# Attention's end reordered: a fourth home for residual rows, the last blocks' values behind more mixing steps, and turned v issued by GpSimd

## The chip, the cores and the metric

One core of a Trainium2 chip. The time is device microseconds (us) of one launch of the whole kernel. Engines are named as in the profile: PE (TensorE), DVE (VectorE), ACT (ScalarE), POOL (GpSimd), SP (SyncE, which here issues nearly all DMAs). "L76" is line 76 of the kernel.

## The reference

A trunk of two layers on one sequence of 1024 tokens, width 1024, in float32. Layer 0 mixes with a gated MLP and a gated delta rule; layer 1 with differential attention of 8 heads. The part around which the change lies, cut to what matters:

```python
h = h + concatenate([a_out, b_out]) @ w_out_e        # layer 0's mixing; then MLP and gate
...
q, k, v = split(rms_norm(h) @ w_qkv)                 # layer 1: 8 heads, two score maps each
attn = softmax(q1 k1) - lam * softmax(q2 k2)         # causal, with linear position bias
o = rms_norm(attn @ v, sub_gain) * (1 - lam_init)    # per head and token
h = h + o @ w_out_o                                  # the output projection ("mixing")
h = h + square(relu(rms_norm(h) @ w_mlp1)) @ w_mlp2  # then the gate
```

## The kernel before, in words

Every large product is made from float32 values split in a rounded part `hi` and a rest `lo`, so each product of a 128x128 weight block with 512 tokens is three PE matmuls (`mm3`): hi x hi, hi x lo, lo x hi. ScalarE makes `hi` (a cast), VectorE or GpSimd makes `lo` (a subtraction). Tokens are handled in two halves of 512.

**Order of the work.** The code issues instructions in program order; a planner then orders each engine's queue from its own model of times, by priority (program order, unless `high_priority` lifts a stretch of code) among what it takes to be ready. On the chip each queue runs strictly in that order, and waits where an operand is not there. `Ordered` (L40) wraps PE: `behind(inst, mark)` forces an instruction to come after another in the plan, `pe.floor` puts all matmuls issued while it is set behind a mark, and `pe.mark` is the last matmul issued. A Tile pool hands out memory by tag: a new tile of a tag waits until the last one in that home is done with.

**Attention** (`attention`, L887) runs 64 blocks, g = 8 x head + b, block b having b + 1 key tiles of 128. In turn g it issues block g's first map of scores (`logits(0)`), then for block g-1 the sum of both maps (`combine`, L1051 on VectorE) and `transpose` (L1056 on VectorE, 32x32 squares, then a DMA on SP to `a_dram`, L1058), for block g-2 `fetch` (L1067: one or two DMAs on SP that read `a_dram` back as `aT` with the squares in place), then `logits(1)`, and for block g-3 `value` (PE matmuls `po<-v,aT`). `value` ends with ScalarE copies (L1078, L1080) and, after every fourth block, the length factor of four blocks: small VectorE operations (L1087 to L1090: `osq`) and three GpSimd ones (L1092 to L1094). For heads 0 to 6 the scaled rows go to DRAM (`o_dram`); head 7's stay.

Between these parts `pump()` is called four times a turn. It draws the projections for later heads from a stream, and from the 206th call on one step of `tails()`. That generator turns six heads' rows of a token half (`put_halves`, `put_o`: PE transposes `tr<-ident,ol`, ScalarE `ohi` L1104, VectorE `olo` L1105), then runs `mix_part` for that half: the output projection over the first KA = 6 (half 0) or 5 (half 1) heads. `mix_part` makes 8 slices m of 128 output features, each 3 matmuls per head, and yields after every second head. It closes slice m behind the second head of slice m+1: VectorE adds the residual rows `res` (L1219), a DMA writes them to `h_dram` (L1220), and the load of slice m+2's rows is issued (L1209) into the next home, three homes in turn: tiles `c0`, `c1`, `c4`. What is left of `tails()` after turn 65 is drawn at once, then head 7's first half is turned.

`attention` returns two functions, kept in `close`: block 63's `value`, and the turning of head 7's second half. The top level then calls `mix_out` (L1237) for half 0 over the heads left (2 heads x 3 x 8 slices), pops the first function after step 8 (slice 3) and the second after step 16 (slice 7), and calls `mix_out` for half 1 (3 heads, of which heads 5 and 6 go first in slices 0 and 1). Each finished slice is added to `acc`, read from `h_dram` (L1249, L1266), squared by ScalarE (the first into the tile `sqs0` for half 0, L237) and summed by VectorE (L241). PSUM tiles of these products come from the tags in `wide`, two tiles each: `mm` and `tr`. The MLP follows.

**Turned v** (`turn`, L1399, layer 0): the values for the delta rule are transposed in 32x32 squares by VectorE (L1402) and written token by token to DRAM in four DMAs of 64 KB on ScalarE's queue (L1405); `(i, hf) == (2, 1)` is v's second half. `read_tokens` (L1411) reads them on SP for the scan's chunks.

Of the kernel before, what the change touches and what calls it, by code (L numbers as in the profile page):

```python
# [11 lines left out]
F32 = mybir.dt.float32  # L12
F32R = mybir.dt.float32r
AF = mybir.ActivationFunctionType
ALU = mybir.AluOpType
# [3 lines left out]
P = 128  # L19
D = 1024  # L20
S = 1024
KT = D // P
NT = S // P
HT = 512
# [5 lines left out]
EARLY = 3000  # L30
LAG = 3
KA = (6, 5)
MARKS = ((64, 50), (192, 144), (212, 160), (227, 168))
TAIL = 205
FILLA, FILLB, FILLC = 36, 60, 48
IDLE = 5
FILLS = (23, 23, 23, 23, 28, 28, 28, 28)
# [2 lines left out]
def f32(ap):  # L40
    return ap.bitcast(F32)
# [73 lines left out]
class Trunk:  # L115
# [771 lines left out]
    def attention(self, w_qkv, w_out, gain_next, h_dram):  # L887

        nc = self.nc
        NB = NT  # L890
        hs, r = list(self.hs), list(self.r)
        self.mixed = [[None] * KT, [None] * KT]
        self.res_home = itertools.cycle(("c0", "c1", "c4"))

        al = self.slot("B", [P, S], F32, "al")
        nc.gpsimd.iota(al, pattern=[[1, S]], base=-(S - P), channel_multiplier=-1, allow_small_or_imprecise_dtypes=True)
# [115 lines left out]
        class Block:  # L1012
# [40 lines left out]
            def transpose(me):  # L1053

                n, nk = me.n, me.b + 1
                nc.vector.transpose(me.lg[0][:, :n], me.lg[1][:, :n])  # L1056
                a_dram = self.dp.tile([nk, P, P], F32, name=self.nm("a_dram"))
                nc.sync.dma_start(a_dram.rearrange("k p c -> p k c"), me.lg[0][:, :n].rearrange("p (k c) -> p k c", c=P))  # L1058
                me.src = a_dram.rearrange("k (i r) (j c) -> k (r j) i c", r=32, c=32)

            def fetch(me):
                nk = me.b + 1
                me.aT = []
                for k0 in range(0, nk, 4):
                    k1 = min(nk, k0 + 4)
                    aT = self.attn_tile(next(aT_tag))
                    self.pe.behind(nc.sync.dma_start(aT[:, : (k1 - k0) * P].rearrange("p (k i c) -> p k i c", i=4, c=32), me.src[k0:k1].rearrange("k p i c -> p k i c")), self.pe.mark)  # L1067
                    me.aT.append(aT)
# [29 lines left out]
        def put_o(hd, hf, o):  # L1098
            pt = self.aux([P, HT], "tr", "tr")
            for t in range(4):  # L1100
                self.pe.transpose(pt[:, t * P : (t + 1) * P], o[:, t, :], self.ident)
            hi = self.hp.tile([P, HT], F32R, tag=f"hi{hf}{hd}", name=self.nm("ohi"))
            lo = self.hp.tile([P, HT], F32R, tag=f"lo{hf}{hd}", name=self.nm("olo"))
            nc.scalar.activation(hi, pt, AF.Copy, scale=self.sg)  # L1104
            nc.vector.scalar_tensor_tensor(lo, pt, self.sg, f32(hi), ALU.mult, ALU.subtract)  # L1105
            self.mixed[hf][hd] = (hi, lo)

        def put_halves():
# [17 lines left out]
        qks, vs, os = [[] for _ in range(8)], [], [[] for _ in range(8)]  # L1126
# [14 lines left out]
        def pump():  # L1141
            i = state[0] = state[0] + 1
            for (i0, u0), (i1, u1) in zip(marks, marks[1:]):
                if i0 < i <= i1:
                    want = u0 + (u1 - u0) * (i - i0) / (i1 - i0)
                    while state[1] < want:
                        next(fill)
                        state[1] += 1
            if i > TAIL:
                next(tail, None)  # L1150
# [11 lines left out]
            yield from puts  # L1162

        tail = tails()
        blocks = []
        for g in range(8 * NB + 2):
            if g < 8 * NB:
                hd, b = divmod(g, NB)
                blocks.append(Block(hd, b))
                blocks[g].logits(0)  # L1170
            if 0 < g <= 8 * NB:
                blocks[g - 1].combine()
                blocks[g - 1].transpose()
            pump()
            if 1 < g <= 8 * NB:
                blocks[g - 2].fetch()
            if g < 8 * NB and b % 2 and b < NB - 1:
                q = heads[hd][2]((b + 1) // 2)
            pump()
            if g < 8 * NB:  # L1180
                if b == 3 - (hd < 7):
                    heads[hd][1](1)
                blocks[g].logits(1)
            pump()
            if g == 8 * NB:
                blocks[g - 1].fetch()
            if g > 2:
                blocks[g - 3].value()
            pump()
            if g < 8 * NB:  # L1190
                if b % 2 and b < NB - 1:
                    heads[hd][3] = q
                if b == 6 and hd < 7:
                    begin(hd + 1)
        for _ in tail:
            pass
        put_o(7, 0, os[7][0])

        return blocks[8 * NB - 1].value, lambda: put_o(7, 1, os[7][1])


    def mix_part(self, h, n, w_out, h_dram):
        nc = self.nc
        cols = slice(h * HT, (h + 1) * HT)

        def load(m):
            if m < KT:
                res = self.slot(next(self.res_home), [P, HT], F32, "res")
                nc.sync.dma_start(res, h_dram[m, :, cols])  # L1209
                ahead.append(res)  # L1210

        ahead, open_ = [], []
        load(0)
        load(1)

        def close():
            m, ps = open_.pop(0)
            res = ahead.pop(0)
            self.pe.behind(nc.vector.tensor_tensor(res, res, ps, ALU.add), self.pe.mark)  # L1219
            nc.sync.dma_start(h_dram[m, :, cols], res)  # L1220
            load(m + 2)

        for m in range(KT):
            if m % 2 == 0:
                w = self.weight(w_out[0 : n * P, m * P : (m + 2) * P], n, 256, nc.gpsimd)
            ps = self.mm_ps()
            for k in range(n):
                self.mm3(ps, w.at(k, slice((m % 2) * P, (m % 2 + 1) * P)), self.mixed[h][k], k == 0, k == n - 1)
                if m and k == 1:
                    close()  # L1230
                if k % 2:
                    yield
            open_.append((m, ps))
        close()
# [65 lines left out]
    def even_mix(self, first, rows_of_rest, rest_of_x, w_in, ws, bs, conv, a_log, dt_bias, v_gain, o_gain, masks, w_out, gain_next, h_dram):  # L1300
        nc = self.nc
# [20 lines left out]
        hs, r, rb = self.hs, self.r, self.rb  # L1322
# [23 lines left out]
        hb, beta, g = small["hb"], small["beta"], small["g"]  # L1346
# [46 lines left out]
        qkv, made, by_token = {}, set(), {}  # L1393
# [5 lines left out]
        def turn(i, hf, m, y):  # L1399

            t = self.sp.tile([P, HT], F32, tag=f"sqs{m % 2}", name=self.nm("turned"), bufs=1)
            nc.vector.transpose(t, y)  # L1402
            for a in range(4):
                f0 = m * P + 32 * a
                nc.scalar.dma_start(by_token[i, hf].rearrange("(t c) f -> c t f", c=32)[:, :, f0 : f0 + 32], t[32 * a : 32 * a + 32].rearrange("c (t r) -> c t r", r=32))  # L1405

        def read_tokens(i, c, out):

# [539 lines left out]
        f0 = prep(0)  # L1948
# [16 lines left out]
def trunk(tc, x, p, ln_mix_e, w_in_e, gmlp_v_gain, gmlp_ws, gmlp_bs, gdn_conv, gdn_a_log, gdn_dt_bias, gdn_out_gain,  # L1965
          w_out_e, ln_mix_o, w_qkv_o, attn_q_gain, attn_k_gain, diff_lambda, attn_sub_gain, w_out_o, ln_mlp, w_mlp1,
          w_mlp2, ln_ple, w_ple_gate, w_ple_proj, masks, out):
    with ExitStack() as ctx:
        T = Trunk(tc, ctx)
        nc = tc.nc  # L1970
# [25 lines left out]
        pt = T.aux_ps()  # L1996
# [24 lines left out]
        T.even_mix(first, rows_of_rest, rest, w_in_e[0], gmlp_ws[0], cols[:, 96:100], conv, gdn_a_log[0], gdn_dt_bias[0], gmlp_v_gain[0], gdn_out_gain[0], masks, w_out_e[0], gain[1], h_dram)  # L2021
        T.attn_consts(attn_q_gain[0], attn_k_gain[0], diff_lambda[0], attn_sub_gain[0], lam_init)
        for layer in range(2):
            T.wide = ("mm", "tr")
            accs = [None] * 4

            def acc_of(m, h):
                i = 2 * h + m // 4
                if accs[i] is None:
                    accs[i] = T.slot(f"A{i ^ 2 * layer}", [P, 4, HT], F32, "acc")  # L2030
                return accs[i][:, m % 4]


            if layer:
                T.new_hs()
                for n, _ in enumerate(T.mix_out(0, lambda m: acc_of(m, 0), w_out_o[0], h_dram, gain[4], KA[0])):
                    if n + 1 in (4 * (KT - KA[0]), 8 * (KT - KA[0])):
                        close.pop(0)()
            for _ in T.mix_out(1, lambda m: acc_of(m, 1), (w_out_e, w_out_o)[layer][0], h_dram, gain[3 * layer + 1], KA[1] * layer, first=(0, 1) if layer else ()):
                pass  # L2040
            x = [[acc_of(m, 0) for m in range(KT)] if layer else T.x0, [acc_of(m, 1) for m in range(KT)]]
            T.wide = ("mm", "tr", "aux", "sc")
            acc, pT, by_token = T.mlp(x, (("A2", "A3"), ("A0", "A1")) if layer else (("A1", "A0"), ("A2", "A3")), gain[3 * layer + 1], w_mlp1[layer], w_mlp2[layer], gain[3 * layer + 2], h_dram, p[layer, 0], layer == 1)
            T.wide = ("mm", "sc", "tr") if layer else ("mm", "tr")
            if layer:
                T.ple_out(pT, acc, by_token, gain[5], w_ple_gate[1], w_ple_proj[1], out[0])
                break
            T.ple(pT, acc, w_ple_gate[0], w_ple_proj[0], gain[3], h_dram)
            T.wide = ("mm",)
            close = [*T.attention(w_qkv_o[0], w_out_o[0], gain[4], h_dram)]  # L2050
# [41 lines left out]
```

## Time and profile before

| | us |
|---|---|
| median of 3 runs | 2492.01 (2491.54 to 2494.98) |
| the profiled execution | 2494.76 |
| its span, first to last instruction | 2493.1 |
| PE busy in it | 2467.7 (99%) |
| DVE, ACT, POOL busy | 1861.1 (75%), 1287.8 (52%), 314.4 (13%) |
| mean granted PE clock | 0.997 of full |

In the rows below, a timeline row is: start, duration, engine, line, operation, out<-in, shape, count, and in brackets how long the engine had been idle before it and what released it. A row of the waits is: who waited <- for whom, total us, number of times, longest. Matmul durations overlap, since matmuls are pipelined; starts tell the rate. A 128x128 float32 matmul is listed as two.

### The profile page before, as it was taken

The numbers are of one execution on the slowest core, as the hardware profiler recorded it, in microseconds if no ns is written. First come the engines' busy times: TensorE is split into PE (matmuls) and PEld (weight loads), VectorE is DVE, ScalarE is ACT, GpSimd is POOL, SyncE is SP. The second block draws the span as 40 slices with busy tenths as digits, with TensorE's granted clock in tenths as the row PEclk, the third lists the DMA queues.
The fourth block names the chain that finished last, engine by engine and source line by source line (L and its number), as shares of the span: only waits on it lengthen the run. The fifth ranks groups of instructions, "written<-read, shape, count | busy, mean of one in ns | idle before, by whom it ended". The sixth has DMA issues, their size and how long they took to land.

```text
span 2493.1 us, 39832 instructions
## 1 busy us (share of the span) xinstructions
PE 2467.7 (99%) x13567; PEld 2108.4 (85%) x13567; DVE 1861.1 (75%) x3639; ACT 1287.8 (52%) x2588; POOL 314.4 (13%) x288
## 2 busy tenths in 40 slices
PE   9999999999999999999999999998999999999999
PEld 7898898888888887888899999987788888888887
DVE  7777876697677788556578888874886677788677
ACT  6553444565445444444366666663654555445543
POOL 0211231000000000000244434441000000000010
PEclk9999999999999999999999999999999999999999
DMA  8384655457557756553347766888475558657872
GB/s 252 112 252 117 185 151 169 131 192 234 161 177 256 248 167 201 184 168 106 115 121 159 171 161 157 197 216 268 131 231 196 177 177 286 221 183 218 230 243 89
DMA packets 559988, 461.96 MB, mean 185 GB/s; under 512 B 248484, under 2 KB 421544, under 8 KB 559784
## 3 DMA queue, kind: packets, MB, share of 16 engines
q1 hardware_dynamic: 525464, 454.16, 60.5%
q10 hardware_dynamic: 33808, 4.20, 1.1%
q8 instruction: 107, 1.75, 0.3%
q0 software_dynamic: 512, 1.05, 0.1%
q14 instruction: 97, 0.79, 0.1%
HBM read 322.95 MB, written 136.33 MB: 184 GB/s over the span
## 4 chain that ended last, share of the span: by engine, by line
PE 91%; DMA 3%; DVE 2%; SPq 1%; ACT 1%; issue 1%; POOL 0%; ACTq 0%; DVEq 0%; POOLq 0%
PE mm L76 81%; PE po L76 3%; PE qk L76 2%; PE aux L76 2%; DMA h_dram<-res 1%; DMA a_dram<-lg 1%; PE tr L79 1%; DMA diag<-early 0%; PE pks L76 0%; PE pz L76 0%; PE py L76 0%; SPq L1067 0%; PE pkq L76 0%; PE pgm L76 0%; PE aux L79 0%
## 5 line engine op out<-in xcount | busy, mean ns | idle before, releaser
L76 PE MATMUL mm<-g,w 128*128 128x512 f32 x2592 | 603.1, 394 | 0.7 <-DVE g L222 0.5
L221 ACT CAST w<-raw 128x512 fp32r<-128x512 f32 x598 | 364.8, 617 | 442.8 <-PE mm L76 359.0
L76 PEld LDWEIGHTS mm<-g,w 128*128 128x128 f32 x2592 | 486.8, 188 | 114.7 <-issue 1.1
L76 PE MATMUL mm<-hi,w 128*128 128x512 f32 x1728 | 553.7, 397 | 0.0
L76 PE MATMUL mm<-w,hi 128*128 128x256 f32 (+2 forms) x2528 | 503.2, 294 | 1.6 <-ACT t L1519 1.5
L222 DVE TENSOR_TENSOR w<-raw,w 128x512 fp32r<-128x512 f32 (+1 forms) x510 | 348.0, 690 | 164.5 <-ACT w L221 156.7
L76 PEld LDWEIGHTS mm<-w,hi 128*128 128x128 f32 x2528 | 401.7, 188 | 16.3 <-ACT t L1519 1.7
L76 PEld LDWEIGHTS mm<-hi,w 128*128 128x128 f32 x1728 | 324.3, 188 | 73.4 <-ACT u L358 0.3
L76 PE MATMUL mm<-w,lo 128*128 128x256 f32 (+2 forms) x1264 | 368.2, 292 | 0.0
L76 PE MATMUL mm<-lo,w 128*128 128x512 f32 x864 | 340.0, 394 | 0.0
L76 PE MATMUL mm<-t,w 128*128 128x512 f32 x1152 | 270.3, 394 | 1.2 <-ACT w L221 1.2
L76 PEld LDWEIGHTS mm<-t,w 128*128 128x128 f32 x1152 | 216.5, 188 | 51.9 <-ACT w L221 1.6
L76 PEld LDWEIGHTS mm<-w,lo 128*128 128x128 f32 x1264 | 237.9, 188 | 5.8
L76 PEld LDWEIGHTS mm<-lo,w 128*128 128x128 f32 x864 | 162.7, 188 | 36.4
L222 DVE TENSOR_TENSOR g<-graw,g 128x512 fp32r<-128x512 f32 x216 | 147.5, 687 | 11.2 <-DMA gd<-g 7.5
L221 ACT CAST g<-graw 128x512 fp32r<-128x512 f32 x216 | 132.7, 617 | 43.3 <-DMA graw<-gd 14.8
L1043 ACT ACTIVATE lg<-lg,nm 128x128 f32<-128x128 f32 (+7 forms) x128 | 99.2, 775 | 73.7 <-DVE nm L1040 72.9
L222 POOL TENSOR_TENSOR w<-raw,w 128x512 fp32r<-128x512 f32 (+1 forms) x88 | 115.6, 1334 | 146.4 <-ACT w L221 93.2
L258 POOL TENSOR_TENSOR r<-ms,mhalf 128x4 f32<-128x4 f32 x12 | 12.5, 1042 | 936.8 <-DVE ms L256 911.1
L342 ACT ACTIVATE g<-g 128x512 f32<-128x512 f32 x96 | 60.4, 631 | 120.3 <-DVE g L276 116.7
L1040 DVE CUSTOM_DVE_ANT_0 lg<-qk,al 128x512 f32<-128x512 f32 (+3 forms) x128 | 74.8, 587 | 28.2 <-PE qk L76 25.0
L76 PE MATMUL mm<-ohi,w 128*128 128x512 f32 x256 | 88.5, 409 | 2.2 <-DVE acc L1266 1.0
(333 smaller groups left out, 3532.6 us busy)
## 6 DMA issues: line engine op xcount, KB each, us to landing
raw<-in_w_mlp_dram SPq DMA_DIRECT2D x352, 256.0 KB, 3.4
graw<-gd SPq DMA_DIRECT2D x224, 256.0 KB, 2.8
gd<-g SPq DMA_DIRECT2D x192, 256.0 KB, 3.2
raw<-in_w_ple_gate_dram SPq DMA_DIRECT2D x76, 256.0 KB, 3.7
acc<-h_dram SPq DMA_DIRECT2D x64, 256.0 KB, 4.1
keep<-in_w_mlp_dram SPq DMA_DIRECT2D x64, 256.0 KB, 4.5
raw<-in_w_in_e_dram SPq DMA_DIRECT2D x60, 256.0 KB, 3.8
h_dram<-acc SPq DMA_DIRECT2D x48, 256.0 KB, 2.6
```

Source lines behind the costliest of these rows:

```text
L76: self._next(self.engine.matmul(*a, **k))
L79: self._next(self.engine.transpose(*a, **k))
L221: self.nc.scalar.copy(hi, src)
L222: (lo_engine or self.nc.vector).tensor_tensor(lo, src, f32(hi), ALU.subtract)
L258: nc.gpsimd.tensor_tensor(r, ms, self.mhalf[:, 0:4], ALU.pow)
L342: nc.scalar.activation(g, src, AF.Relu)
L1040: nc.vector.tensor_tensor_reduce(out=lg[:, k0:k1], in0=ps[:, : k1 - k0], in1=al[:, u0 + k0 : u0 + k1], scale=-1.0, scalar=3.0e38 if c == 0 ...
L1043: nc.scalar.activation(lg[:, :n], lg[:, :n], AF.Exp, bias=nm[:, r, nch - 1 : nch], scale=-1.0, accum_out=me.sums[:, b, r : r + 1])
```

## The change

Eight edits:

1. Residual rows have four homes in turn, `sqs0` first (the small-pool tile that later holds half 0's sum of squares), then `c0`, `c1`, `c4`.
2. `LATE`: in turns 64 and 65, ahead of `value` of blocks 61 and 62, five and two further steps of `tails()` are drawn, and the matmuls of that `value` are put behind the last of them.
3. Block 63's `combine` and `transpose` are issued with high priority.
4. The `olo` of a head's rows turned after block 63's transpose was issued (the last ones) is put behind that transpose.
5. Block 63's `value`, with its length factor, is issued with high priority, and its matmuls behind the last matmul issued before it.
6. It is called after step 4 (slice 1) of half 0's `mix_out` instead of step 8 (slice 3).
7. In layer 1 `mix_out` may use the PSUM tag `sc` too.
8. The four DMAs of each turned slice of v's second half (16 in all) are issued by GpSimd instead of ScalarE.

```diff
+LATE = {64: 5, 65: 2}
...
-        self.res_home = itertools.cycle(("c0", "c1", "c4"))
+        self.res_home = itertools.cycle(("sqs0", "c0", "c1", "c4"))
...
-                nc.vector.transpose(me.lg[0][:, :n], me.lg[1][:, :n])
+                inst = nc.vector.transpose(me.lg[0][:, :n], me.lg[1][:, :n])
...
+                return inst.ins.name
...
-            nc.vector.scalar_tensor_tensor(lo, pt, self.sg, f32(hi), ALU.mult, ALU.subtract)
+            inst = nc.vector.scalar_tensor_tensor(lo, pt, self.sg, f32(hi), ALU.mult, ALU.subtract)
+            if len(turned) == 8 * NB:
+                self.pe.behind(inst, turned[-1])
...
             if 0 < g <= 8 * NB:
-                blocks[g - 1].combine()
-                blocks[g - 1].transpose()
+                with self.tc.high_priority(EARLY) if g == 8 * NB else contextlib.nullcontext():
+                    blocks[g - 1].combine()
+                    turned.append(blocks[g - 1].transpose())
...
             if g == 8 * NB:
                 blocks[g - 1].fetch()
+            for _ in range(LATE.get(g, 0)):
+                next(tail, None)
+            if g in LATE:
+                self.pe.floor = self.pe.mark
             if g > 2:
                 blocks[g - 3].value()
+            self.pe.floor = None
...
-        return blocks[8 * NB - 1].value, lambda: put_o(7, 1, os[7][1])
+        def last():
+            with self.tc.high_priority(EARLY):
+                self.pe.floor = self.pe.mark
+                blocks[8 * NB - 1].value()
+                self.pe.floor = None
+
+        return last, lambda: put_o(7, 1, os[7][1])
...
-                res = self.slot(next(self.res_home), [P, HT], F32, "res")
+                res = self.attn_tile(next(self.res_home))
...
-                nc.scalar.dma_start(by_token[i, hf]...)
+                (nc.gpsimd if (i, hf) == (2, 1) else nc.scalar).dma_start(by_token[i, hf]...)
...
-            T.wide = ("mm", "tr")
+            T.wide = ("mm", "tr", "sc") if layer else ("mm", "tr")
...
-                    if n + 1 in (4 * (KT - KA[0]), 8 * (KT - KA[0])):
+                    if n + 1 in (2 * (KT - KA[0]), 8 * (KT - KA[0])):
                         close.pop(0)()
```

More of the change, by code (lines that the diff above doesn't have):

```diff
@@ L1164, in attention @@
         tail = tails()
-        blocks = []
+        blocks, turned = [], []
         for g in range(8 * NB + 2):
@@ L1404, in turn @@
                 f0 = m * P + 32 * a
-                nc.scalar.dma_start(by_token[i, hf].rearrange("(t c) f -> c t f", c=32)[:, :, f0 : f0 + 32], t[32 * a : 32 * a + 32].rearrange("c (t r) -> c t r", r=32))
+                (nc.gpsimd if (i, hf) == (2, 1) else nc.scalar).dma_start(by_token[i, hf].rearrange("(t c) f -> c t f", c=32)[:, :, f0 : f0 + 32], t[32 * a : 32 * a + 32].rearrange("c (t r) -> c t r", r=32))
         def read_tokens(i, c, out):
```

## Prediction

> **What bounds the kernel now.** TensorE (PE) is busy nearly all the time, so time can only come out of the few places where it stands still. I read first the table of busy time in equal stretches: of all stretches the 150 us around attention's end (1600 to 1750 us) hold nearly all of PE's idle time, 11.6 us; before that the only idle stretch near an edited line is at 150 to 160 us. Next, the waits of PE between 1600 and 1760 us, longest first (who waited <- for whom: total, times, longest):
>
> ```profile
> PE po L76 <- DMA aT<-a_dram: 3.8, 1, 3.8
> PE tr L79 <- POOL o L1094: 2.5, 1, 2.5
> PE tr L79 <- DVE ks L994: 1.0, 1, 1.0
> PE mm L76 <- DVE acc L1266: 1.0, 1, 1.0
> PE tr L79 <- DMA ol<-o_dram: 1.0, 1, 1.0
> PE qk L76 <- ACT qh L1005: 0.9, 1, 0.9
> PE mm L76 <- DVE res L1219: 0.7, 1, 0.7
> ```
>
> Every one is a single event, so each can be given its place. The waits for `ks` and `qh` belong to the start of head 7 near 1625 us; the diff does not touch them. The others lie in three places, whose price is in the table of stretches (length, then busy of PE, weight loads, VectorE/DVE, ScalarE/ACT, GpSimd/POOL; then granted clock, DMA share, GB/s):
>
> ```profile
> 1680.00:1695.00 15.00, 10.21 (x44) 8.46 (x43) 6.73 (x12) 4.92 (x11) 3.24 (x5) 0.77 0.98 296
> 1708.00:1715.00 7.00, 5.77 (x31) 4.53 (x30) 1.73 (x3) 2.54 (x4) 0.00 (x0) 1.00 0.90 270
> 1735.00:1745.00 10.00, 6.55 (x23) 4.87 (x23) 4.44 (x8) 1.80 (x3) 3.16 (x3) 0.83 0.63 227
> ```
>
> PE idles 15.00 - 10.21 = 4.8 us at place A (block 61's values wait for `aT`), 1.2 us at B (residual rows and a weight late), 3.45 us at C (the last head's last rows wait for their length factor). Around A and C the granted clock falls too: 10.21 busy us at 0.77 lose 2.3 us, 6.55 at 0.83 lose 1.1 us. So A costs 7.1 us, B 1.2 us, C 4.6 us: 12.9 us together.
>
> A skill rule would price C lower. The Trainium skill's page "TensorE: Matmul & The Clock Gate" (section "What's actually happening") has the array go to half clock only after an idle window of about 3.4 us. No single wait at C is longer than 2.5 us, so by the rule C is worth 3.45 us and the sum below 1.1 us less; the 0.83 in the row disagrees, and I go by the row.
>
> Why A waits is in SP's queue, which issues its DMAs strictly in order. Its two largest waits in the same 160 us:
>
> ```profile
> SPq L1067 <- DMA a_dram<-lg: 15.5, 8, 3.0
> SPq L1209 <- DMA h_dram<-res: 15.5, 7, 4.1
> ```
>
> The second is the load of a residual tile that must wait until the same home's last rows have landed in DRAM; three homes make that happen seven times, and everything behind it on SP waits too. The chain of waits then shows the last blocks' round trips through DRAM strung one after another on SP:
>
> ```profile
> 1678.02 5.71 DMA a_dram<-lg
> 1683.79 0.37 SPq L1067
> ...
> 1698.94 4.47 DMA a_dram<-lg
> 1703.43 0.37 SPq L1067
> ```
>
> And the last block is late for a second reason, VectorE's own queue:
>
> ```profile
> 1685.68 1.28 DVE L1051 SCALAR_TENSOR_TENSOR lg<-lg,rs,lg 128x1024 f32<-128x1024 f32 x1
> 1693.48 0.75 DVE L1105 SCALAR_TENSOR_TENSOR olo<-tr,sg,ohi 128x512 fp32r<-128x512 f32 x1 [6.51 <-ACT ohi L1104]
> 1694.15 1.24 DVE L1056 STREAM_TRANSPOSE lg<-lg 128x1024 f32<-128x1024 f32 x1
> ```
>
> Block 63's sum (L1051) was done at 1686.96, but its transpose began at 1694.15, because an `olo` in front of it stood 6.51 us for a transpose that PE held behind place A.
>
> **The change, part by part.** *Values behind more mixing steps (place A).* The unit is one mixing product, from three rows of PE's timeline without a gap:
>
> ```profile
> 1715.10 0.40 PE L76 MATMUL mm<-olo,w 128*128 128x512 f32 x1
> 1715.34 0.63 PE L76 MATMUL mm<-ohi,w 128*128 128x512 f32 x2
> 1715.80 0.39 PE L76 MATMUL mm<-olo,w 128*128 128x512 f32 x1
> ```
>
> Three starts in 0.70 us: 0.233 us each. A slice of the second half's part has 5 heads x 3 = 15 products in two steps (12, then 3 more with the next slice). In the program block 61's values stood behind 3 steps (15 + 6 = 21 products); now behind 8 (3 x 15 + 12 = 57). The 36 products in between are 36 x 0.233 = 8.4 us of work laid over a wait of 3.83 us (plus the 1.0 us for `ol` just ahead). Blocks 61 to 62 then lie 45 products apart (10.5 us; 30 before), 62 to 63 30 products (7.0 us). Against round trips that now end on SP at 1683.8 and 1703.4 us, 8 to 10 us apart, that is enough even if SP gets no faster. Nothing is added: the same products run in another order, so the gain is A's whole 7.1 us, less what is late next (below).
>
> *Fourth home.* It issues no more DMAs. The load for slice m+2 then waits for the write of slice m-2 instead of m-1, one slice (15 to 18 products, 3.5 to 4.2 us) older; SP's 15.5 us at L1209 mostly go. PE does not wait there now, so alone I cost it at nothing; it is what lets the mixing steps pulled forward have their rows. Its new wait: the home `sqs0` is also the sum of squares that ScalarE starts at the first finished slice (L237), with all of ScalarE's casts behind it. The last rows in that home are slice 4 of half 1 (closed 75 + 6 products into that part); the first square comes after 120 + 6 products: 45 x 0.233 = 10.5 us later, against the landing of 5.3 us in the DMA table:
>
> ```profile
> h_dram<-res SPq DMA_DIRECT2D x16, 256.0 KB, 5.3
> ```
>
> So covered; without that cover it would cost 1 us for each us.
>
> *Block 63's sum and transpose first, `olo` behind it.* The 6.5 us in front of the transpose go, and its DRAM round trip starts as much earlier. It is off PE's path now; what it buys is margin for the next part.
>
> *Last values two slices earlier, length factor first (place C).*
>
> ```profile
> 1726.03 0.72 PE L76 MATMUL po<-v,aT 128*128 128x128 f32 x5
> ...
> 1740.31 0.44 PE L79 MATMUL tr<-ident,o 128*128 128x128 f32 x2 [2.48 <-POOL o L1094]
> ```
>
> From block 63's last values to the transpose that they release there are 14.3 us. GpSimd's share is 3.3 us:
>
> ```profile
> 1736.94 1.92 POOL L1092 TENSOR_TENSOR of<-osq,mhalf 128x4 f32<-128x4 f32 x1 [30.85 <-DVE osq L1090]
> 1738.94 0.20 POOL L1093 TENSOR_TENSOR of<-of,c 128x4 f32<-128x4 f32 x1
> 1739.22 1.04 POOL L1094 TENSOR_TENSOR o<-o,of 128x512 f32<-128x512 f32 x1
> ```
>
> The rest is 0.7 us of products, under 1 us of ScalarE and under 1 us of VectorE: about 6 us bare. The other 8 us are queueing behind casts, squares and additions. The program put 36 products behind the last values before the third head is needed (8.4 us), now 48 (11.2 us): with priority on both queues a chain of 6 to 11 us fits. With nothing but the move, 14.3 - 11.2 = 3 us would still show. I take C as gone: 4.6 us. The third PSUM tag (`sc`) takes the 1.0 us `acc` wait, which is in C already.
>
> *B:* 1.2 us, not removed by any edit; I leave it standing (0 to 1.2 us).
>
> *Turned v on GpSimd's queue.* 16 DMAs leave ScalarE for GpSimd.
>
> ```profile
> 150.41 2.22 ACTq L1405 DMA_DIRECT2D by_token<-turned  x4
> 152.67 0.63 ACT L1448 ACTIVATE t<-t 128x512 f32<-128x512 f32 x1 [3.70 <-DMA by_token<-turned]
> ```
>
> ```profile
> 155.50 0.51 PE L76 MATMUL mm<-w,hi 128*128 128x256 f32 x2 [1.49 <-ACT t L1519]
> ```
>
> Four issues held ScalarE 2.2 us, and PE then stood 1.49 us for the next evacuation. VectorE's input to that activation was ready only about 0.8 us before it ran, so I take 0.8 us (0 to 1.5). On GpSimd, idle there, four such DMAs cost 2.56 us where the kernel already does it:
>
> ```profile
> 2396.14 2.56 POOL L516 DMA_DIRECT2D by_token<-t  x4 [0.79 <-DVE t L513]
> ```
>
> *What is late next.* With A gone, the mixing steps run 8 us ahead and need residual rows and weights from an SP that still waits for three round trips. The nearest rows are B's 0.7 (`res`) and 0.5 us (weight); at most A returns there (7 us). I take 2 us.
>
> **Sum:** 7.1 + 4.6 + 0.8 - 2.0 = 10.5 us. The profiled execution took 2494.8 us (span 2493.1), so 2484.3 by it; the three runs' median is 2492.0, 2.8 us lower, so I predict **2481.5 us**.
>
> **Rivals.** *A comes back in the mixing steps.* DMA share at A is 0.98, and SP issues `aT` of block 63 ahead of later residual loads; a VectorE addition for such a row already stood 9.3 us. If PE stops there for what it now waits at A, only C and the early part are gained: 4.6 + 0.8, about 2486.5. Against it: the fourth home frees SP.
>
> ```profile
> DVE res L1219 <- DMA res<-h_dram: 9.3, 1, 9.3
> ```
>
> *It does not do what it says.* Priorities act on the order that a planner makes from its own durations; if the real waits outrun them as now, the chain at C stays long and A only shifts: about 2491.
>
> *Slower: VectorE's queue blocks.* Block 63's length factor stands first on VectorE; if the planner sets it before the values are really there, all behind it waits: the additions that free PSUM. Six banks of 6 products are 6 x 1.4 = 8.4 us of cover. Beyond that each us is lost, and the kernel is slower than now from 8.4 + 10.5 = 19 us on, twice the 9.3 us above: about 2498 at 25 us.
>
> *GpSimd's DMAs starve.* The read of turned v is at its limit:
>
> ```profile
> SPq L1411 <- DMA by_token<-turned: 3.2, 1, 3.2
> ```
>
> ```profile
> 280.00:300.00 20.00, 20.00 (x174) 18.74 (x172) 15.72 (x39) 7.32 (x17) 5.27 (x6) 1.00 0.75 204
> 2390.00:2410.00 20.00, 20.00 (x92) 16.43 (x91) 18.09 (x31) 9.32 (x17) 10.63 (x17) 1.00 0.89 271
> ```
>
> If GpSimd could issue only while VectorE rests (4.3 us of 20 here, for 2 x 2.56 = 5.1 us), the last piece lands some 5 us late and the scan's next chunk with it: about 2486. The Trainium skill's page "SBUF — State Buffer" (section "SBUF: two separate sides") warns of this: VectorE can lock GpSimd out of writing descriptors. The second row disagrees: four issues took 2.56 us with VectorE 18.09 of 20 us busy.
>
> *More than forecast.* If head 7's start and B also smooth out: about 2477.
>
> **How the numbers follow.** Forecast (2478 to 2485) 0.60; A returns 0.16; no effect 0.06; slower 0.05; starved 0.03; more 0.10. The range 2476 to 2488 leaves out no effect, slower and the tails of two others, under 0.2. What a measurement can tell from no change is about 0.2%, 5 us, so faster means under 2487.0: 0.60 + 0.10 + 0.02 and 0.09 of A's return, 0.81; within 0.14; slower 0.05.
>
> **What would show it.** Right: no wait of `po` for `aT` over 1 us; `tr` no longer waiting for GpSimd's `o`; SP's wait at L1209 near zero; block 63's transpose right behind its sum; PE idle under 5 us and the clock at 1.00 after head 7's start. Wrong: PE waiting for `res` or a weight for several us between the last values; VectorE standing at `osq`; the read of `by_token` later than 3 us against its place now. The forecast fails if the stretch from 1680 to 1750 us does not shrink by 8 to 13 us.

## The result and the profile after

| | before | after |
|---|---|---|
| median, us (22 runs each) | 2492.51 (2489.64 to 2496.22) | 2489.27 (2484.85 to 2493.46) |
| the profiled execution, its span | 2494.76, 2493.1 | 2488.19, 2486.5 |

The ratio is 0.9984 (95% interval 0.9977 to 0.9991): about 4 us faster by the ratio, 3.2 us by the medians, against the forecast 10.5. The two traces differ by 6.6 us, since the trace of before is 2.2 us above its median and that of after 1.1 us below. Lines after the edits are shifted: the additions of residual rows are L1235 (their tile is now called `aT`), their loads L1225, block 63's transpose L1057, the scaling of the MLP's rows L1298 and its cast L1302.

The waits of PE in after, 1590 to 1760 us:

```profile
PE mm L77 <- ACT hi L1302: 3.3, 1, 3.3
PE tr L80 <- DMA ol<-o_dram: 2.2, 1, 2.2
PE tr L80 <- DVE ks L995: 1.0, 1, 1.0
PE qk L77 <- ACT qh L1006: 0.9, 1, 0.9
PE qk L77 <- DVE nm L1041: 0.2, 1, 0.2
```

The 3.8 us for `aT`, the 2.5 us for GpSimd's `o` and the waits for `acc` and `res` are gone. Two things stand in their place: the wait for `ol` grew from 1.0 to 2.2 us, and there is a new wait of 3.3 us for a cast `hi` that nobody waited for before. The table of stretches of after shows where that is:

```profile
1735.00:1745.00 10.00, 10.00 (x49) 8.32 (x48) 8.69 (x15) 5.74 (x11) 1.39 (x1) 1.00 0.83 294
1745.00:1765.00 20.00, 16.67 (x74) 13.47 (x73) 16.50 (x28) 10.85 (x19) 1.01 (x1) 0.91 0.35 105
1600.00:1760.00 160.00, 152.36 (x812) 130.06 (x812) 120.26 (x256) 87.46 (x197) 43.86 (x38) 0.97 0.83 234
```

Place C (1735 to 1745) is full, at clock 1.00. Right behind it PE idles 3.3 us and then runs at a lower clock. It is the door of the MLP. PE's timeline there, first of before, then of after (`aux<-ones,sqs` makes the sums of squares of half 0, called sums below; `aux<-ident,r`, called rows below, spreads the norm's factors over rows; `mm<-hi,w` is the MLP's first product):

```profile
1745.38 0.95 PE L76 MATMUL aux<-ones,sqs 128*128 128x1 f32 x8
1752.08 1.05 PE L76 MATMUL aux<-ident,r 128*128 128x128 f32 x8
1758.06 0.62 PE L76 MATMUL mm<-hi,w 128*128 128x512 f32 x2
```

```profile
1738.89 0.95 PE L77 MATMUL aux<-ones,sqs 128*128 128x1 f32 x8
1745.80 1.05 PE L77 MATMUL aux<-ident,r 128*128 128x128 f32 x8
1750.19 1.63 PE L77 MATMUL mm<-hi,w 128*128 128x512 f32 x4 [3.33 <-ACT hi L1302]
```

In before, 6.0 us lie between the spread factors and the first MLP product, filled with 22 mixing products (22 x 0.233 = 5.1 us). In after the spread factors are PE's very last work before the MLP: of the 384 mixing products none is left to cover the chain that follows. That chain, from the timelines of ScalarE and VectorE in after:

```profile
1746.89 0.58 ACT L267 COPY rb<-aux 128x512 f32<-128x512 f32 x1 [0.33 <-PE aux L77]
...
1749.52 1.28 ACT L1302 CAST hi<-acc 128x512 fp32r<-128x512 f32 x2 [1.51 <-DVE acc L1298]
```

```profile
1746.93 0.69 DVE L223 TENSOR_TENSOR w<-raw,w 128x512 fp32r<-128x512 f32 x1
1747.54 0.69 DVE L242 TENSOR_TENSOR sqs<-sqs,t 128x512 f32<-128x512 f32 x1
1748.14 0.68 DVE L223 TENSOR_TENSOR w<-raw,w 128x512 fp32r<-128x512 f32 x1
1748.74 1.41 DVE L1298 SCALAR_TENSOR_TENSOR acc<-acc,cols,rb 128x512 f32<-128x512 f32 x2
```

The chain is a copy, 1.3 us behind an addition of squares and a weight's split on VectorE, the scaling, the cast: 4.4 us from the start of the spreading to the first product. In the order of before it is hidden; here it stands bare.

My theory at that point: A and C are gone as forecast, but the way in which C went put the chain from half 0's squares to the MLP's first operand at the end of PE's order, and 3.3 us of wait plus half clock are paid there. Rivals: the loss is in the early part (turned v); it is in the fourth home and SP's queue; or the move of the last values is no gain in itself.

### The profile page after: what moved, and what is told of

It is laid out like the page before. It is cut to its first block, busy times and chain, and to the rows that moved or that the text cites. A ratio compares the mean times of both kernels' runs of the same rounds, so it can differ in the third digit from the quotient of the medians.

```text
span 2486.5 us, 39842 instructions
## 1 busy us (share of the span) xinstructions
PE 2466.9 (99%) x13567; PEld 2107.8 (85%) x13567; DVE 1862.4 (75%) x3639; ACT 1288.3 (52%) x2588; POOL 324.2 (13%) x304
## 4 chain that ended last, share of the span: by engine, by line
PE 94%; DVE 3%; DMA 2%; issue 1%; ACT 0%; SPq 0%; POOL 0%; DVEq 0%; ACTq 0%; POOLq 0%
PE mm L77 82%; PE po L77 3%; PE qk L77 3%; PE aux L77 2%; PE tr L80 1%; DVE acc L277 1%; DMA raw<-in_w_mlp_dram 0%; DVE raw L277 0%; PE pkq L77 0%; PE pz L77 0%; PE py L77 0%; PE aux L80 0%; PE pks L77 0%; PE pgm L77 0%; PE pvn L77 0%
## 5 line engine op out<-in xcount | busy, mean ns | idle before, releaser
L259 POOL TENSOR_TENSOR r<-ms,mhalf 128x4 f32<-128x4 f32 x12 | 12.9, 1074 | 949.9 <-DVE ms L257 922.8
```

The lines of the kernel that those rows point to most:

```text
L259: nc.gpsimd.tensor_tensor(r, ms, self.mhalf[:, 0:4], ALU.pow)
```

## The experiments

Each run against the kernel before (ratio with its 95% interval; us = ratio less 1, times 2492.5). Each four rows in turn were run side by side on one chip, with 5 runs for the two rows named 'all, rows forced' and 7 to 12 for the others:

| run | median | ratio | us |
|---|---|---|---|
| turned v alone | 2490.55 | 0.9991 (0.9982 to 0.9999) | -2.2 |
| last values alone | 2494.57 | 1.0003 (0.9995 to 1.0012) | +0.7 |
| all but the last values | 2486.87 | 0.9975 (0.9966 to 0.9984) | -6.2 |
| all, rows forced | 2483.75 | 0.9964 (0.9953 to 0.9976) | -9.0 |
| forced, `ol` behind | 2486.70 | 0.9978 (0.9968 to 0.9988) | -5.5 |
| forced, last values late | 2485.24 | 0.9970 (0.9959 to 0.9981) | -7.5 |
| forced, three homes | 2488.60 | 0.9984 (0.9975 to 0.9992) | -4.0 |
| forced, no extra steps | 2486.15 | 0.9974 (0.9965 to 0.9983) | -6.5 |
| the change again | 2487.06 | 0.9976 (0.9967 to 0.9984) | -6.0 |
| all, rows forced, again | 2481.30 | 0.9954 (0.9942 to 0.9967) | -11.5 |
| forced, `ol` behind, again | 2488.09 | 0.9982 (0.9973 to 0.9991) | -4.5 |
| last values alone, rows forced | 2489.77 | 0.9988 (0.9979 to 0.9997) | -3.0 |

**Turned v alone.** The kernel before with one line of the diff:

```diff
-                nc.scalar.dma_start(by_token[i, hf]...
+                (nc.gpsimd if (i, hf) == (2, 1) else nc.scalar).dma_start(by_token[i, hf]...
```

> The kernel before with one edit: the sixteen by_token DMAs of part (2,1) issued by GpSimd. Theory (places A and C are gone, but C's wait had covered the chain that feeds the MLP's first product): the early edit is worth what the early landmarks of the pair of traces say, about 2 us: 2490.0 to 2491.5 against 2492.5, PE's 1.49 us wait for ScalarE's t at 155 us gone, nothing else changed. Rival (the lost gain is lost early, the edit gives nothing or costs): 2492 to 2494, with PE waiting elsewhere before 300 us.

Measured 2.2 us (0.2 to 4.5): the theory's size, and PE's wait for ScalarE's `t` is gone. The traces agree: PE's idle time from 100 to 330 us is 2.7 us in before (first row) and 0.3 us here (second row).

```profile
100.00:330.00 230.00, 227.26 (x1826) 207.29 (x1826) 177.88 (x458) 107.61 (x252) 54.83 (x63) 1.00 0.63 179
100.00:330.00 230.00, 229.73 (x1857) 210.05 (x1856) 182.40 (x469) 108.49 (x257) 64.15 (x78) 1.00 0.63 178
```

The early part holds no loss. This trace is worth more for another thing. Around attention's end PE's order is that of before, and still that stretch looks better (waits, then stretches):

```profile
PE po L76 <- DMA aT<-a_dram: 3.6, 1, 3.6
PE tr L79 <- POOL o L1094: 2.5, 1, 2.5
```

```profile
1680.00:1700.00 20.00, 16.44 (x85) 13.92 (x84) 8.12 (x13) 6.97 (x16) 4.86 (x5) 0.91 0.96 260
1700.00:1735.00 35.00, 31.27 (x143) 24.72 (x143) 19.51 (x34) 11.97 (x25) 4.55 (x5) 1.00 0.97 308
```

The same two waits, but A costs 3.56 + 0.09 x 16.44 = 5.0 us and B and C together 3.73 us with no loss of clock: 8.8 us, where the one execution that I had priced gave 12.9.

**Last values alone**: edits 5, 6 and 7 without the rest:

```diff
-LATE = {64: 5, 65: 2}
+LATE = {}
...
-        self.res_home = itertools.cycle(("sqs0", "c0", "c1", "c4"))
+        self.res_home = itertools.cycle(("c0", "c1", "c4"))
```

(and block 63's sum and transpose, `olo` and turned v as before).

> Only the edits on the last block's values: two slices earlier, first on VectorE, third PSUM tag; three homes, no extra mixing steps, no priority for block 63's sum and transpose, by_token on ScalarE. Theory: place A stays (po waits 3 to 4 us for aT); the 2.5 us wait of tr for GpSimd's o goes, and in its place the MLP's first product waits 2 to 3.5 us for hi, since that chain's length does not change: 2491 to 2493, 0 to -1.5 us. Rival (C is a clean gain and the loss of the whole change lies elsewhere): -4.6 us, 2488, no wait for hi above 0.5 us.

No gain (+0.7 us, -1.2 to +3.0), and the new wait has taken C's place with about its length, 3.3 us for 3.45:

```profile
PE po L77 <- DMA aT<-a_dram: 3.6, 1, 3.6
PE mm L77 <- ACT hi L1302: 3.3, 1, 3.3
PE mm L77 <- DVE aT L1235: 1.8, 1, 1.8
```

As the theory had it; the rival of a clean gain of 4.6 us is out.

**All but the last values**: the change with edits 5 and 6 undone.

```diff
-        return last, lambda: put_o(7, 1, os[7][1])
+        return blocks[8 * NB - 1].value, lambda: put_o(7, 1, os[7][1])
...
-                    if n + 1 in (2 * (KT - KA[0]), 8 * (KT - KA[0])):
+                    if n + 1 in (4 * (KT - KA[0]), 8 * (KT - KA[0])):
```

> The changed kernel with the last block's values called where they were before (two slices later, no priority). Theory: A stays gone; the last rows' transpose waits again for GpSimd's o, 1.5 to 3.5 us, and under that wait the sums, rows, scaling and cast catch up, so the wait for hi falls below 1 us: the time is that of the changed kernel within 1.5 us, 2488 to 2490.5. Rival (C's gain is real and kept in the changed kernel): 4.6 us slower than the changed kernel, about 2494. Second rival (the loss is the fourth home and SP): same as the changed kernel, with the wait for hi still at 3 us.

The median, 2486.87, lies below the range of the theory; by the ratios it is 2.2 us faster than the whole change, and 0.2 us against the change's second run (below), both within the noise. `tr` did not wait for GpSimd's `o` in this execution, and the theory was right on the wait for `hi` only in part: it fell to 0.6 us, but a product right behind it waited 1.8 us for `lo`, the rest that goes with `hi`.

```profile
1751.66 1.20 PE L77 MATMUL mm<-hi,w 128*128 128x512 f32 x4 [0.55 <-ACT hi L1302]
1754.64 0.80 PE L77 MATMUL mm<-lo,w 128*128 128x512 f32 x1 [1.78 <-DVE lo L1303]
```

So the MLP's door still costs 2.3 of the 3.3 us of idle time here. What the run does show is that on top of the other edits the move of the last values has no gain that can be measured, and that the rival of a kept gain of 4.6 us is out. It doesn't rule out the fourth home as the cause, since that home is in this kernel too; the next runs decide that.

**Rows forced.** The edit touches the order of PE alone (the planner then orders the other engines' queues anew): half 0's sums before slice 3 and rows before slice 5 of half 1's last products, and those slices behind them.

```diff
-            if h == 1 and k0 and m in (2, 4):
+            if h == 1 and k0 and m in (3, 5):
                 self.pe.floor = self.pe.mark
                 self.later.pop(0)()
-                self.pe.floor = None
+                self.pe.floor = self.pe.mark
```

(the floor is lifted behind the last slice).

> The changed kernel, with sums, rows and the products of the second half's last slices in a forced order: sums after 339 of the 384 mixing products (358 in the changed kernel's plan), rows after 357 (384). Theory: the operands were ready by then (the last square of the first half was added at 1734.1 us, product 337), so rows and the casts behind them come about 6 us earlier, the 3.3 us wait for hi falls below 0.5 us and the 1.8 us of half clock behind it go too: 2484 to 2486, that is 3 to 5 us under the changed kernel, 6 to 8 under the kernel before. Rival (VectorE's and ScalarE's additions and casts are the limit, the order of PE does not matter): no gain, the wait only moves to sums or rows, 2488 to 2490.

The change and the forced rows were later run once more, beside each other:

> The changed kernel once more, for a second trace of it and for times on the same chip as the next three. Theory: 2488 to 2490.5; in the trace the first product of the MLP waits again about 3.3 us for hi (the order of the engines fixes that wait), while the waits for ol, for x at the start and for ScalarE's t near 155 us come and go by 1 to 2 us. Rival (that wait was an accident of one execution): under 1.5 us this time.

> The forced rows once more: five runs gave 2483.75, too few to be sure of the last us. Theory: 3 to 5.5 us under the changed kernel of this same call, no wait for hi over 0.5 us. Rival (five lucky runs, the forced order is worth under 2 us): within 2 us of the changed kernel.

The change again has the same wait of 3.3 us in its second trace, so it is no accident. The forced order is 5.5 us under it where both ran on one chip (0.9954 against 0.9976, uncertain by some 4 us by the two intervals), and its first runs are 5 us under the result above (0.9964 against 0.9984). PE's timeline in the first trace with the forced rows:

```profile
1736.89 1.05 PE L77 MATMUL aux<-ones,sqs 128*128 128x1 f32 x8 [0.46 <-DVE sqs L242]
1742.07 1.05 PE L77 MATMUL aux<-ident,r 128*128 128x128 f32 x8
1749.20 0.62 PE L77 MATMUL mm<-hi,w 128*128 128x512 f32 x2
```

The sums now wait 0.46 us for the last square, so they cannot come much earlier; 7.1 us of products lie over the chain, and the MLP starts without a wait. PE, VectorE, ScalarE and GpSimd have as many instructions as in after (13567, 3639, 2588 and 304): the order of some products is worth 5 to 5.5 us. With the fourth home kept, this rules that home out as the cause of this loss.

**Last values alone, rows forced**: the second run with that same edit.

> The edits on the last block's values alone (as in the run with only these, 2494.57) and the forced order of sums and rows. Theory: C is a gain of 3 to 4.6 us as soon as the chain behind it is early: the wait for hi goes, and the time is 3 to 6 us under the run with these edits alone: 2488.5 to 2491.5, at last under the kernel before's 2492.7. Rival (the move of the last values is a loss by itself, not through the chain behind it): 2493 to 2495 as without the forced order.

3.7 us under the second run (uncertain by some 3 us). The wait for `hi` is gone, and what was no gain has become 3.0 us (0.7 to 5.2). That bears the theory out: the move at C is worth something when the chain behind it is early. The forced order was not run on the kernel before without the move, so its own share of the 3.0 us isn't shown; next to the other edits it is 1.2 us without the move (-7.5 against -6.2 us in the table).

**What each part is worth with the rows forced.** Three runs take one part out (`LATE = {}`; the old call of block 63's values; three homes), one, run twice, holds the turnings of (0,6) and (1,6) behind half 1's mixing products:

```diff
+            self.pe.floor = self.pe.mark
             yield from puts
+            self.pe.floor = None
```

> The kernel with the forced rows, without the seven mixing steps pulled ahead of blocks 61 and 62. Theory: place A returns with one wait of po for aT of 3 to 4 us and half clock behind it, less the ol waits that it has now: 1.5 to 4 us slower than 2483.75, 2485 to 2488. Prediction's price of A: 7.1 us slower, 2491. Rival (A is worth nothing, since ol waits took its place): within 1 us of 2483.75.

> The kernel with the forced rows, but the last block's values called where they were before. Theory: with the rows out of the way the earlier values have a worth of their own, and without them the last rows' transpose waits for GpSimd's o again: 2 to 4.6 us slower than the forced rows, 2486 to 2488.5. Rival (the last values' move is worth nothing whatever stands behind it): 2483 to 2485, no wait for o.

> The kernel with the forced rows and three homes for residual rows in place of four. The prediction's step (the fourth home lets the mixing steps have their rows): slower by 2 to 5 us, 2486 to 2489, with PE or VectorE waiting for residual rows between 1670 and 1710. Theory now (SP waited 14.9 us for homes in the changed kernel against 15.5 before, so the fourth home moved little): within 1 us of 2483.75.

> The kernel with the forced rows, and the turnings of (0,6) and (1,6) held behind the second half's mixing products. Theory (what is left at place A is three waits for ol, 4.6 us idle between 1680 and 1700 us with the clock at 0.91, because the mixing products that could stand there are in the order behind those turnings): the ol waits go, the stretch 1680 to 1700 is busy over 19 us at clock 1.00, and the time falls by 3 to 6 us against the forced rows' 2483.75: 2478 to 2481. Rival (the residual rows and aT behind the same queue of SP are as late, so the wait only gets another name): the idle time in that stretch stays over 3 us, 2483 to 2485.

> Forced rows with the turnings of (0,6) and (1,6) behind the second half's mixing products, again beside the forced rows on one chip. If place A's idle time only took another name (waits for ol in the one, for residual rows in the other), the two lie within 1.5 us of each other. If the turnings held behind are a real loss, as the first medians had it (2486.7 against 2483.75), it is 2 to 4 us slower again; if the trace is right (stretch of attention's end 131.7 us against 133.6), 1 to 2 us faster.

They stand against the mean of the two runs with forced rows, -10.2 us, which ran on other chips; by the intervals each difference is uncertain by some 3 us. Without the extra steps 3.7 us are lost (the theory's 1.5 to 4, not the 7.1 that I had for A), and `po` waits 3.6 us for `aT` again. With the late last values 2.7 us are lost, the theory's size (2 to 4.6) but not clear of the noise, and the median of 2485.24 is below the expected range; `tr` waits for `o` again:

```profile
PE tr L80 <- POOL o L1096: 2.5, 1, 2.5
```

The fourth home was a miss: 6.2 us, not under 1. I had taken SP's wait for homes, hardly changed by the fourth (after, 1590 to 1760 us; 15.5 in before), as the measure of what a home is worth:

```profile
SPq L1225 <- DMA h_dram<-aT: 14.9, 7, 3.3
```

Part of the price stands elsewhere, in PE's waits; first with three homes, then with four (second run with forced rows):

```profile
PE mm L77 <- DVE aT L1235: 4.9, 2, 2.8
PE tr L80 <- DVE lg L1057: 1.7, 1, 1.7
```

```profile
PE mm L77 <- DVE aT L1235: 0.8, 1, 0.8
```

With three homes the additions of residual rows come late, hold PSUM, and PE waits 4.9 us for them. But with four homes PE waits there for other things: its idle time from 1680 to 1735 us is 6.6 us with three homes and 4.8 and 4.6 us in the two traces with four. So about 2 of the 6.2 us have a place in the traces; where the rest lies, they do not show. How long SP waits for a home did not tell here whether the rows still come in time.

With the `ol` turnings held behind, I was wrong too: 4.7 us slower, and 5.7 in the repeat (7.0 against the forced rows that ran beside it). PE's timeline of the repeat, its idle rows from 1700 to 1715 us:

```profile
1704.83 0.47 PE L77 MATMUL mm<-ohi,w 128*128 128x512 f32 x1 [1.50 <-DVE aT L1237]
1710.76 0.50 PE L77 MATMUL mm<-ohi,w 128*128 128x512 f32 x1 [2.25 <-DVE aT L1237]
```

The waits for `ol` go, and products that run ahead in their place meet residual rows that are not there: the wait gets another name, as the rival said. That explains that nothing was gained; the loss beyond it these runs leave open. Whether the rows are late because of SP's order or because the DMA engines are full (share 0.94 to 1.01 in these stretches) was not tried either.

## Why the prediction was wrong, point by point

- **What bounds the kernel.** The 11.6 us of PE's idle time around attention's end are not nearly all of it: the profile has 2493.1 - 2467.7 = 25.4 us in the whole span.
- **Place A** (forecast 7.1 us). Removed as described: no wait of `po` for `aT` is left in after (0.9 us in the run without the move of the last values). Size wrong: taking the extra steps out costs 3.7 us, not 7.1. Part of the price was one execution's wait and clock (5.0 us in another trace with the same order). That execution was also 2.8 us slower than the median from which the forecast took the whole price off. Part came back as waits of what stands in A's place, near to the first rival, though for `ol` and not for residual rows: 2.2 us in after, more in the first trace with forced rows:

```profile
PE tr L80 <- DMA ol<-o_dram: 4.6, 3, 2.1
```

- **Place B** (left standing, 0 to 1.2 us). Its waits, for `res` and for a weight, are not in after's list.
- **Fourth home** ("alone at nothing; lets the mixing steps have their rows"). The second half is right: beside the extra steps and the forced rows the home is worth 6.2 us. Alone it was not run. The sign I looked for, SP's wait near zero, was the wrong one: it stayed at 14.9 us.
- **Block 63's transpose right behind its sum.** Nearly: VectorE's timeline of after has an `olo` and an addition between, 1.2 us instead of 7.2:

```profile
1686.03 1.29 DVE L1052 SCALAR_TENSOR_TENSOR lg<-lg,rs,lg 128x1024 f32<-128x1024 f32 x1
1687.23 0.75 DVE L1107 SCALAR_TENSOR_TENSOR olo<-tr,sg,ohi 128x512 fp32r<-128x512 f32 x1
1687.89 0.68 DVE L1235 TENSOR_TENSOR aT<-aT,mm 128x512 f32<-128x512 f32 x1
1688.49 1.24 DVE L1057 STREAM_TRANSPOSE lg<-lg 128x1024 f32<-128x1024 f32 x1
```

- **Place C** (4.6 us). The wait went as forecast, and the change got nothing for it that can be measured: with the planner's order the move loses 0.2 to 2.2 us beside A and 0.7 alone, all within the noise. With the rows forced it gains 2.7 us beside A, not clear of the noise either, and 3.0 alone, the forced order's own share included.
- **Turned v** (0.8, at most 1.5). 2.2 us, so probably mis-sized low: the interval of 0.2 to 4.5 us holds 0.8 too, but the idle time from 100 to 330 us fell by 2.5 us in the trace of turned v alone. GpSimd issued its four DMAs in 2.79 us, and the read of `by_token` waited 2.8 us at most against 3.2, so they did not starve:

```profile
150.73 2.79 POOL L1421 DMA_DIRECT2D by_token<-turned  x4 [6.34 <-DVE turned L1418]
```

```profile
SPq L1427 <- DMA by_token<-turned: 3.8, 3, 2.8
```

- **What is late next** (2.0 us). This is the step that failed. I looked for the next wait only among the products that move forward, at their residual rows and weights, and did not follow the second consumer behind C: the MLP's first operand. It is 3.3 us of wait and 1.7 to 2.9 us of half clock, 5.0 to 6.2 us for which the sum held nothing (its 2.0 us stood for residual rows and weights), and undoing it alone gave 5 to 5.5 us. I also took PE's order behind C as given; the planner had moved sums and rows 21 and 22 products later. Why its model did so was not tried.

With that wait forced away the time is 2483.75 and 2481.3 us, beside the 2481.5 predicted for the change. That one of them comes so near is luck: it is another kernel, and errors offset each other, since A and C are worth less than I had, and turned v (probably) and the fourth home more.

## What to carry to other kernels

When a stall on the bounding engine goes, list everything that ran during the stall, not only what waited at its end, and ask of each next consumer how many instructions still cover it; count them in the order of the engine, before and after. A planner that orders queues by its own times may put work of no cost last, where it has no cover: the position of a short chain's first instruction is worth checking after each reordering. And price a wait from more than one execution: the same order of PE's work cost 12.9 us in one trace and 8.8 in another.

## What the runs showed of the hardware

The price of a gap depends on more than its length. The same wait of 3.3 us for `hi` cost 1.7 us of clock in the one trace of after (rows below: 0.36 x 2.0 + 0.49 x 2.0) and 0.11 x 26.66 = 2.9 us in the other:

```profile
1750.20:1752.20 2.00, 2.00 (x6) 1.50 (x7) 2.00 (x4) 0.75 (x2) 0.00 (x0) 0.64 0.40 124
1752.20:1754.20 2.00, 2.00 (x7) 1.52 (x6) 2.00 (x4) 1.08 (x2) 0.00 (x0) 0.51 0.00 0
1754.20:1756.20 2.00, 2.00 (x10) 1.64 (x9) 2.00 (x4) 0.98 (x2) 0.00 (x0) 1.00 0.00 0
```

```profile
1735.00:1765.00 30.00, 26.66 (x117) 21.87 (x116) 22.75 (x39) 16.27 (x30) 2.39 (x2) 0.89 0.44 145
```

The Trainium skill's page "TensorE: Matmul & The Clock Gate" (section "What's actually happening") says that the gate looks at windows of 3413 ns that run freely. The first trace agrees in one thing: its rows make (0.36 + 0.49) x 2.0 / 0.5 = 3.4 us at half clock. The other makes 2.9 / 0.5 = 5.9 us, more than one such window, and the gap itself, 3.3 us, is shorter than one. That the two prices come from where the gap falls in the windows would fit, but no run here shows where they lie. And 3.5 us of idle time in three gaps of at most 1.3 us (second run with forced rows) cost no clock at all, while three gaps of 1.4, 1.2 and 2.1 us in the same stretch of the first run with forced rows (second row) went with a clock of 0.91:

```profile
1680.00:1700.00 20.00, 16.53 (x87) 13.60 (x88) 10.13 (x17) 7.83 (x16) 6.55 (x6) 1.00 0.94 260
1680.00:1700.00 20.00, 15.38 (x69) 11.94 (x68) 9.87 (x17) 7.59 (x13) 4.84 (x6) 0.91 0.95 258
```
